# A two-layer decoder trunk on one core: 1/rms multiplied into U, another root and two banks for the last norm, the last two tiles stored one by one

## The chip, the core and the metric

The kernel runs on one core of a Trainium2 chip. TensorE (PE) multiplies matrices into eight PSUM banks, VectorE (DVE) and ScalarE (ACT) work on what comes out, GpSimd (POOL) helps with work that needs no PSUM, and SyncE (SP) issues most DMAs. Each engine takes its instructions from its own queue, in order, so an instruction that waits holds up all that stand behind it. The metric is the device time of one execution in microseconds, lower is better.

## The reference

The input `x` has 256 tokens of 1024 features. Two layers follow each other, each a mixer and an MLP, and a last norm ends the program:

```python
for layer in range(DEPTH):
    h = rms_norm(x, mix_norm[layer])
    x = x + (gdn_shortconv_mixer if layer % 2 == 0 else nsa_mixer)(h, ...)
    x = x + squared_relu_mlp(rms_norm(x, mlp_norm[layer]), w_up[layer], w_down[layer])
return rms_norm(x, final_norm)

def rms_norm(x, w):
    y = x * lax.rsqrt(jnp.mean(x * x, axis=-1, keepdims=True) + NORM_EPS)
    return y * w
def squared_relu_mlp(h, w_up, w_down):
    return jnp.square(jax.nn.relu(h @ w_up)) @ w_down
```

The MLP is 1024 to 4096 to 1024. Since relu is homogeneous, `relu((x*r) @ W)` is `relu(x @ W) * r` for the positive factor r = 1/rms of a token, and its square is `relu(x @ W)**2 * r**2`.

## The kernel before

Everything is held transposed, with features on the 128 partitions and the 256 tokens along a row: the residual stream `X` is eight tiles of 128x256. Precision is kept by splitting: each weight and each activation becomes a high part and a low part (`uh` and `ul` for the weights, `x[:, m, 0]` and `x[:, m, 1]` or `U[:, m, 0]` and `U[:, m, 1]` for the activations), and a product is three matmuls (`mm256`). A weight unit of 128x1024 is loaded by SP into a stage buffer (`st`), ACT copies it into `uh`, and DVE subtracts to get `ul` (for some units ACT and a DMA that accumulates do it). There are four unit buffers (`UB = 4`), so the split of a unit begins when PE is done with the unit four before it.

A norm does not wait with its result: PE multiplies by `x * w` without 1/rms, and the factor is applied behind. `Norm.ready(m)` splits a tile of `X` as it appears and squares it on ACT (`sq`), POOL or DVE adds the squares up (`nacc`). When the eighth is in, `Norm.finish` lets PE sum over the partitions with `ones`, DVE makes the mean (`ms`) and the root (`rsqrt`, eight small instructions on 128x2 numbers, result `ncol`), PE transposes the column into a row across all partitions (matmuls `b<-par,ncol`), and ACT copies that row out of PSUM (`rbc`). For the last norm (`self.last`) the sum is taken from `nacc` and the eighth `sq` apart, the bank of rows is kept (`n4.rows`), POOL has multiplied `X` by the weight beforehand, and `store` multiplies by the rows and issues the output DMAs in four groups of two tiles (`STORE`): groups on DVE read the bank, the group listed in `GST` runs on POOL and reads `rbc`.

In `mlp` the up projection makes 32 tiles of 128x256; the first four come together from `proj_ko`, the others one by one from `proj_m`. `evac` takes relu from PSUM on ACT (`t`), squares it (`u`), copies the high part to `U`, and DVE subtracts the low part. The down projection makes eight tiles of 96 matmuls each; `down` multiplies by `r2`, the square of `rbc`, and adds to `X`, two DVE instructions.

The order of every queue is fixed before the program runs: a small planner (`Order`) walks through all the streams with its own costs, picks the next instruction, and for some instructions picks the engine (a dict of engines after `yield`). So an edit in one place can change the order and the engines of everything that is planned later. In `mlp` and behind it, streams ask for a bank (`BANK`), for a token (`take`) or for a flag; `n.rbc` is there when the flag `norm1` or `norm3` is set.

Of the kernel before, what the change touches and what calls it, by code (L numbers as in the profile page):

```python
# [10 lines left out]
F32 = mybir.dt.float32  # L11
# [3 lines left out]
AF = mybir.ActivationFunctionType  # L15
# [5 lines left out]
T = 256  # L21
# [6 lines left out]
XBIAS, DBIAS, XB0 = 300, -400, 1e9  # L28
GM, GT, GO = 2, 1, 1
HEAD, CL = 0, 0  # L30
STORE, GST = (0, 2, 4, 6, 8), (2,)
FIRST, XS = (1,) * 8, ((1, 2), (2, 4), (4, 6), (6, 8))
PK, PW, PR, F1, GZ, ZP, LD, RT, P2 = 1, 1, 1, 1, 1, 1, 1, 21, 8
KPOOL, VPOOL, QPOOL, CVB = (), (), (0, 1, 2, 3), {'conv': 4, 'pool': 2}
# [129 lines left out]
class Order:  # L164
# [28 lines left out]
    def flag(self, name):  # L193
        self.flags.setdefault(name, self._now())
# [103 lines left out]
        self.t, self.last, self.hold = (parent.t, parent.last, parent.hold) if parent else (0.0, None, 0.0)  # L298


TABLES = {AF.Exp: ('e',), AF.Ln: ('l',), AF.Silu: ('s',), AF.Tanh: ('e', 's')}


class Timed:
# [61 lines left out]
BANK = ('bank',)  # L366
UB, SB, SPARE1 = 4, 8, 0
SLOTS, PTS = 4, 4
WARM, KEEP, KMAX = 11, 900.0, 8
ONE, WO, HALF, SOFT, TURN, VH = 1, 0, (0, 1), None, None, 1  # L370

# [17 lines left out]
def _build(ctx, nc, tc, wts, xin, parin, out, off):  # L389
# [380 lines left out]
    class Norm:  # L770
# [8 lines left out]
        def ready(self, m):  # L779
            w = self.w[:, m:m + 1]  # L780
            if self.acc is None:
                self.acc = tmp.tile([128, T], F32, name="nacc", bufs=1)
                if not self.last:
                    x = actp.tile([128, KT * 2 * T + 64], F32R, name="x")[:, 16:16 + KT * 2 * T]
                    self.x = x.rearrange("p (k a t) -> p k a t", k=KT, a=2)
            if not self.last:
                pick = yield dict(A=400, V=261 + (XBIAS if self.idx else XB0))
                if pick == 'A':
                    A.activation(self.x[:, m, 0], X[:, m], AF.Copy, scale=w)
                else:  # L790
                    V.tensor_scalar(self.x[:, m, 0], X[:, m], w, None, op0=OP.mult)
                yield 'V'
                V.scalar_tensor_tensor(self.x[:, m, 1], X[:, m], w, self.x[:, m, 0].bitcast(F32),
                                       op0=OP.mult, op1=OP.subtract)
                flag(f'n{self.idx}x{m}')
            self.begun += 1
            first = self.begun == 1
            if not first:
                yield 'take', 'sq', 3
            yield 'A'  # L800
            self.count += 1
            last = self.count == KT
            sq = self.acc if first else tmp.tile([128, T], F32, name="sq", bufs=3)
            A.activation(sq, X[:, m], AF.Square)
            if first:
                flag(f'n{self.idx}first')
            else:
                yield 'flag', f'n{self.idx}first'
                if last:
                    yield 'flag', f'n{self.idx}sum'  # L810
                    spawn(self.finish(sq), 0)
                else:
                    pick = yield dict(V=334) if not self.idx else dict(G=687)
                    (V if pick == 'V' else G).tensor_add(self.acc, self.acc, sq)
                    order.give('sq')
                    self.sums += 1
                    if self.sums == KT - 2:
                        flag(f'n{self.idx}sum')
            if self.last:
                yield 'G'  # L820
                G.tensor_mul(X[:, m], X[:, m], w.to_broadcast([128, T]))
                flag(f'xw{m}')

        def finish(self, sq):
            if not self.last:
                yield 'V'
                V.tensor_add(self.acc, self.acc, sq)
                order.give('sq')
            parts = [self.acc, sq] if self.last else [self.acc]
            yield 'flag', 'par2'  # L830
            ss = yield BANK
            yield 'PE'
            if self.last:
                keep(ss)
            for i, x in enumerate(parts):
                for t in range(2):
                    PE.matmul(ss[:, t:t + 1], x[:, t * 128:t * 128 + 128], ones, start=(t == 0 and i == 0),
                              stop=(t == 1 and x is parts[-1]))
            yield 'V'
            ms = tmp.tile([128, 2], F32, name="ms")  # L840
            V.tensor_scalar(ms, ss[:, :2], 1.0 / D, EPS, op0=OP.mult, op1=OP.add)
            release(ss)
            self.col = const.tile([128, 2], F32, name="ncol", bufs=2)
            rsqrt(self.col, ms, 2)
            flag(f'col{self.idx}')
            rb = yield BANK
            yield 'PE'
            if self.last:
                keep(rb)
            for t in range(2):  # L850
                PE.transpose(rb[:, t * 128:t * 128 + 128], self.col[:, t:t + 1].to_broadcast([128, 128]), ident)
            if self.last:
                self.rows = rb[:, :T]
                flag('rows')
            yield 'A'
            self.rbc = const.tile([128, T], F32, name="rbc", bufs=2)
            A.activation(self.rbc, rb[:, :T], AF.Copy)
            if not self.last:
                release(rb)
            flag(f'norm{self.idx}')  # L860

    def main():
        n0 = Norm(0)

        def start(m):
            yield 'flag', f'x{m}'
# [10 lines left out]
        n3 = Norm(3)  # L877
        yield from layer1(e, n2, n3)
        n4 = Norm(4, last=True)
        yield from mlp(e, n3, n4)  # L880

        def store(i, a, b):
# [19 lines left out]
def mlp(e, n, nxt):  # L902
    tc, tmp, X, order = e.tc, e.tmp, e.X, e.order
    V, A, PE, G = e.eng
    with tc.tile_pool(name="up", bufs=1) as up:
        U = up.tile([128, 32, 2, T], F32R, name="U")

        def evac(base):
            def f(m, acc):
                yield 'take', 'mlp', 3  # L910
                yield 'A'
                t = tmp.tile([128, T], F32, name="t", bufs=3)
                A.activation(t, acc[:, :T], AF.Relu)
                order.release(acc)
                u = up.tile([128, T], F32, name="u", bufs=3)
                A.activation(u, t, AF.Square)
                A.activation(U[:, base + m, 0], u, AF.Copy)
                yield 'V'
                V.tensor_sub(U[:, base + m, 1], u, U[:, base + m, 0].bitcast(F32))
                order.flag(f'U{n.idx}.{base + m}')  # L920
                order.give('mlp')
            return f

        yield from e.proj_ko(n, evac(0), wide=False)
        yield from e.proj_m(n.x, 28, evac(4))
        r2 = tmp.tile([128, T], F32, name="r2", bufs=1)

        def square():
            yield 'flag', f'norm{n.idx}'
            yield 'V'  # L930
            V.tensor_mul(r2, n.rbc, n.rbc)
            order.flag(f'r2.{n.idx}')

        order.spawn(square())

        def down(m, acc):
            yield 'flag', f'r2.{n.idx}'
            yield 'take', 'mlp', 3
            t = tmp.tile([128, T], F32, name="t", bufs=3)
            yield 'V'  # L940
            V.tensor_mul(t, acc[:, :T], r2)
            order.release(acc)
            V.tensor_add(X[:, m], X[:, m], t)
            order.give('mlp')
            order.spawn(nxt.ready(m))

        for m in range(KT):
# [1064 lines left out]
```

## Time and profile before

| what | us |
|---|---|
| median of three runs | 683.12 (681.45 to 685.27) |
| the profiled execution | 681.15 |
| its span, first to last instruction | 679.4 |
| PE busy in it | 659.2 |
| DVE, ACT, POOL busy | 455.9, 402.1, 119.9 |

The granted TensorE clock is 0.998 of full speed over the span. The stages by time from the start of the span: the first mixer to 182 us, the first MLP to about 356 us, attention to about 480 us, the second MLP to 668 us, and then the last norm and the output. Nearly all instructions are recorded by one helper, so they carry the line number L314 and are told apart by their tiles: `b` is any PSUM bank, `t<-b` the relu, `X<-X,b` a residual add or the last norm's multiplication.

### The profile page before, as it was taken

Reading aid. Unit: us, or ns where it says so; the run is one execution under the profiler, and the core shown is the slowest. Engines: PE = TensorE matmul, PEld = TensorE weight load, DVE = VectorE, ACT = ScalarE, POOL = GpSimd, SP = SyncE. Lnnn points to the kernel's source line nnn. Section 1 sums busy time; section 2 is a strip of 40 time slices with the busy share of each in tenths; the row PEclk is TensorE's granted clock in tenths of the full one; section 3 lists DMA queues with packets and bytes.
Section 4 is the critical chain, followed back from the end, with each engine's and each line's share of the span. In section 5 each row is a group of like instructions: output and inputs, shape, how many; then the busy total and the mean of one; then the engine's idle time right before and its main releaser. Section 6 shows DMA issues by size and latency. Waiting matters only on the chain.

```text
span 679.4 us, 16247 instructions
## 1 busy us (share of the span) xinstructions
PE 659.2 (97%) x6641; PEld 626.7 (92%) x6641; DVE 455.9 (67%) x871; ACT 402.1 (59%) x781; POOL 119.9 (18%) x159
## 2 busy tenths in 40 slices
PE   8999889999999999999999999998999999999995
PEld 6999789999999999999999877886899999999994
DVE  6999677586855655555557998887576555645552
ACT  7565223234888776444457678788578788544430
POOL 1001666410300000001033521021220000012121
PEclk9999999999999999999999999999999999999999
DMA  8961523136566666666658558362456555655401
GB/s 292 315 220 32 159 67 96 61 95 197 176 189 195 199 193 190 195 196 197 191 171 186 176 200 261 132 187 63 119 195 214 187 189 199 202 187 190 152 1 63
DMA packets 33770, 114.33 MB, mean 168 GB/s; under 512 B 3872, under 2 KB 4128, under 8 KB 33696
## 3 DMA queue, kind: packets, MB, share of 16 engines
q1 hardware_dynamic: 31968, 107.53, 50.4%
q0 software_dynamic: 1440, 5.24, 3.9%
q8 instruction: 52, 0.85, 0.5%
q10 hardware_dynamic: 288, 0.52, 0.2%
q14 instruction: 22, 0.18, 0.1%
HBM read 106.99 MB, written 1.05 MB: 159 GB/s over the span
## 4 chain that ended last, share of the span: by engine, by line
PE 80%; DVE 11%; ACT 4%; issue 2%; DMA 1%; SPq 0%; DVEq 0%; ACTq 0%
PE b L314 80%; DVE ul L314 3%; ACT uh L314 1%; DMA st<-wts 1%; ACT px L314 1%; DVE cvconv L314 1%; DVE rqt L314 1%; DVE kc L314 1%; DVE swq L314 1%; SPq L461 0%; DVE lc L314 0%; ACT E L314 0%; DVE qr L314 0%; DVE nm L314 0%; DVE preconv L314 0%
## 5 line engine op out<-in xcount | busy, mean ns | idle before, releaser
L314 DVE TENSOR_TENSOR ul<-st,uh 128x1024 fp32r<-128x1024 f32 (+3 forms) x194 | 228.2, 1179 | 152.7 <-ACT uh L314 150.8
L314 ACT ACTIVATE uh<-st 128x1024 fp32r<-128x1024 f32 (+3 forms) x204 | 206.4, 1013 | 200.9 <-PE b L314 166.6
L314 PE MATMUL b<-x,uh 128*128 128x256 f32 x1664 | 294.4, 281 | 0.6 <-issue 0.5
L314 PEld LDWEIGHTS b<-x,uh 128*128 128x128 f32 x1664 | 251.4, 188 | 3.7 <-issue 0.9
L314 PE MATMUL b<-x,ul 128*128 128x256 f32 x832 | 231.1, 278 | 1.6 <-DVE ul L314 1.1
L314 PE MATMUL b<-U,uh 128*128 128x256 f32 x1024 | 174.2, 276 | 0.0
L314 PEld LDWEIGHTS b<-x,ul 128*128 128x128 f32 x832 | 156.4, 188 | 2.8 <-DVE ul L314 2.1
L314 PEld LDWEIGHTS b<-U,uh 128*128 128x128 f32 x1024 | 154.0, 188 | 0.0
L314 PE MATMUL b<-U,ul 128*128 128x256 f32 x512 | 141.3, 276 | 0.0
L314 PEld LDWEIGHTS b<-U,ul 128*128 128x128 f32 x512 | 96.1, 188 | 0.0
L314 POOL TENSOR_TENSOR nacc<-nacc,sq 128x256 f32<-128x256 f32 x24 | 29.9, 1246 | 242.4 <-ACT sq L314 241.9
L314 ACT ACTIVATE px<-b,nm 128x128 f32<-128x128 f32 (+1 forms) x64 | 26.6, 440 | 3.5 <-DVE nm L314 3.4
L314 ACT ACTIVATE U<-u 128x256 fp32r<-128x256 f32 x64 | 26.8, 419 | 2.0
L314 ACT ACTIVATE u<-t 128x256 f32<-128x256 f32 x64 | 26.7, 418 | 2.0
L314 DVE TENSOR_TENSOR U<-u,U 128x256 fp32r<-128x256 f32 x64 | 27.0, 424 | 0.7 <-ACT U L314 0.7
L314 PE MATMUL b<-uh,x 128*128 128x264 f32 (+1 forms) x128 | 24.5, 288 | 0.0
L314 PE MATMUL b<-ohl,uh 128*128 128x256 f32 x128 | 23.9, 287 | 0.2
L314 ACT ACTIVATE t<-b 128x256 f32<-128x256 f32 x64 | 23.3, 364 | 0.0
L314 POOL TENSOR_TENSOR X<-X,par 128x256 f32<-128x256 f32 x8 | 5.5, 691 | 100.8 <-ACT nacc L314 91.8
L314 PEld LDWEIGHTS b<-uh,x 128*128 128x128 f32 x128 | 20.3, 188 | 0.0
L314 PEld LDWEIGHTS b<-ohl,uh 128*128 128x128 f32 x128 | 19.5, 188 | 0.7 <-ACT ohl L314 0.3
L314 ACT ACTIVATE sq<-X 128x256 f32<-128x256 f32 x35 | 13.5, 404 | 10.6 <-DVE X L314 10.5
(275 smaller groups left out, 797.6 us busy)
## 6 DMA issues: line engine op xcount, KB each, us to landing
st<-wts SPq DMA_DIRECT2D x188, 512.0 KB, 3.7
ul<-st POOLq DMA_DIRECT2D x10, 512.0 KB, 4.8
st<-wts SPq DMA_DIRECT2D x8, 280.0 KB, 2.9
st<-wts SPq DMA_DIRECT2D x8, 264.0 KB, 5.9
st<-wts SPq DMA_DIRECT2D x8, 256.0 KB, 6.3
X<-xt SPq DMA_DIRECT2D x3, 256.0 KB, 6.1
par<-par SPq DMA_DIRECT2D x1, 525.0 KB, 6.7
out_dram<-X SPq DMA_DIRECT2D x2, 256.0 KB, 2.6
```

The costliest lines, as they stand in the source:

```text
L314: r = f(*a, **k)
```

## The change

It has three parts. In `mlp`, relu and the product with 1/rms become one DVE instruction that reads the bank and `n.rbc`, so `U` holds the finished activation; `r2` and its product go, and `down` is one addition from the bank. In the last norm, the root is a DVE reciprocal, an ACT `Sqrt`, and one Newton step of three DVE instructions; `ACT` loads the table for `Sqrt` early, in a stream `root` that waits for `norm3`; and the row across partitions is made twice, in two banks, one for DVE and one for ACT's copy. In `store`, the last group of two tiles becomes two groups of one. (Two constants, `SQ0` and `NA0`, are brought in with the values that the code had.)

```diff
-STORE, GST = (0, 2, 4, 6, 8), (2,)
+STORE, GST = (0, 2, 4, 6, 7, 8), (2,)
...
+SQ0, NA0 = 'A', dict(V=334)
...
 # Norm.finish
-            rsqrt(self.col, ms, 2)
+            if self.last:
+                y = tmp.tile([128, 16], F32, name="rqt", bufs=3)
+                V.reciprocal(y[:, :2], ms)
+                yield 'A'
+                A.activation(y[:, 2:4], y[:, :2], AF.Sqrt)
+                yield 'V'
+                V.tensor_mul(y[:, 4:6], y[:, 2:4], y[:, 2:4])
+                V.scalar_tensor_tensor(y[:, 4:6], y[:, 4:6], -0.5, ms, op0=OP.mult, op1=OP.mult)
+                V.scalar_tensor_tensor(self.col, y[:, 4:6], 1.5, y[:, 2:4], op0=OP.add, op1=OP.mult)
+            else:
+                rsqrt(self.col, ms, 2)
...
             if self.last:
                 self.rows = rb[:, :T]
                 flag('rows')
+                rb = yield BANK
+                yield 'PE'
+                for t in range(2):
+                    PE.transpose(rb[:, t * 128:t * 128 + 128], self.col[:, t:t + 1].to_broadcast([128, 128]), ident)
...
+        def root():
+
+            yield 'flag', 'norm3'
+            yield 'A'
+            A.activation(tmp.tile([128, 1], F32, name="tb", bufs=3), ones, AF.Sqrt)
...
 # mlp
                 yield 'take', 'mlp', 3
+                yield 'flag', f'norm{n.idx}'
+                yield 'V'
+                t = tmp.tile([128, T], F32, name="t", bufs=3)
+                V.scalar_tensor_tensor(t, acc[:, :T], 0.0, n.rbc, op0=OP.max, op1=OP.mult)
+                order.release(acc)
                 yield 'A'
-                t = tmp.tile([128, T], F32, name="t", bufs=3)
-                A.activation(t, acc[:, :T], AF.Relu)
-                order.release(acc)
...
         def down(m, acc):
-            yield 'flag', f'r2.{n.idx}'
-            yield 'take', 'mlp', 3
-            t = tmp.tile([128, T], F32, name="t", bufs=3)
             yield 'V'
-            V.tensor_mul(t, acc[:, :T], r2)
+            V.tensor_add(X[:, m], X[:, m], acc[:, :T])
             order.release(acc)
-            V.tensor_add(X[:, m], X[:, m], t)
-            order.give('mlp')
             order.spawn(nxt.ready(m))
```

The first place is the start of the second MLP, right behind the root of its norm. DVE's queue there, before (`ul` is the low part of a weight unit, `U` the low part of an activation tile):

```order
L314 SCALAR_TENSOR_TENSOR ncol<-rqt,ncol 128x2
L314 TENSOR_TENSOR U<-u,U 128x256 x3
L314 TENSOR_TENSOR ul_7108<-st,uh_7107 128x1024
L314 TENSOR_TENSOR U<-u,U 128x256
L314 TENSOR_TENSOR ul_7150<-st,uh_7149 128x1024
```

The same place of DVE's queue with the change, where `t<-b,rbc` is the new instruction:

```order
L314 SCALAR_TENSOR_TENSOR ncol<-rqt,ncol 128x2
L314 TENSOR_TENSOR ul_7075<-st,uh_7074 128x1024
L314 SCALAR_TENSOR_TENSOR t<-b_6903,rbc 128x256
L314 SCALAR_TENSOR_TENSOR t<-b_6904,rbc 128x256
L314 SCALAR_TENSOR_TENSOR t<-b_6905,rbc 128x256
L314 TENSOR_TENSOR ul_7117<-st,uh_7116 128x1024
L314 TENSOR_TENSOR U<-u,U 128x256 x2
L314 SCALAR_TENSOR_TENSOR t<-b_6906,rbc 128x256
L314 SCALAR_TENSOR_TENSOR t<-b_7067,rbc 128x256
L314 TENSOR_TENSOR ul_7155<-st,uh_7154 128x1024
```

Before, three tiles had been taken out of PSUM by ACT and stood ready for their subtraction; now the first three leave PSUM here, behind `rbc`, and their subtractions come a unit later. ACT's queue at this place, with the change:

```order
L314 ACTIVATE uh_7074<-st 128x1024
L314 ACTIVATE rbc<-b_7077 128x256
L314 ACT_TABLE_LOAD
L314 ACTIVATE tb<-ones 128x1
L314 ACTIVATE uh_7116<-st 128x1024
L314 ACTIVATE u<-t 128x256
L314 ACTIVATE U<-u 128x256
L314 ACTIVATE u<-t 128x256
L314 ACTIVATE U<-u 128x256
L314 ACTIVATE uh_7154<-st 128x1024
```

The table load and the first `Sqrt` stand between `rbc` and the next weight unit; there is no table load behind them to the end of ACT's queue.

The second place is the end of the program. DVE's last instructions before (the branch that ends the queue left out):

```order
L314 TENSOR_TENSOR t<-b_9027,r_8141 128x256
L314 TENSOR_TENSOR X<-X,t 128x256
L314 TENSOR_SCALAR ms<-b_9140 128x2
L314 TENSOR_SCALAR ncol<-ms 128x2
L314 TENSOR_TENSOR rqt<-ncol 128x2
L314 TENSOR_TENSOR rqt<-rqt,ms 128x2
L314 SCALAR_TENSOR_TENSOR rqt<-rqt 128x2
L314 SCALAR_TENSOR_TENSOR ncol<-rqt,ncol 128x2
L314 TENSOR_TENSOR rqt<-ncol 128x2
L314 SCALAR_TENSOR_TENSOR rqt<-rqt,ms 128x2
L314 SCALAR_TENSOR_TENSOR ncol<-rqt,ncol 128x2
L314 TENSOR_TENSOR X<-X,b_9163 128x512 x3
```

With the change (`rqt<-ms` is the reciprocal; ACT's `Sqrt` stands between it and the next):

```order
L314 TENSOR_TENSOR X<-X,b_8996 128x256
L314 TENSOR_SCALAR ms<-b_9106 128x2
L314 RECIPROCAL rqt<-ms 128x2
L314 TENSOR_TENSOR rqt<-rqt 128x2
L314 SCALAR_TENSOR_TENSOR rqt<-rqt,ms 128x2
L314 SCALAR_TENSOR_TENSOR ncol<-rqt 128x2
L314 TENSOR_TENSOR X<-X,b_9124 128x512 x2
L314 TENSOR_TENSOR X<-X,b_9124 128x256 x2
```

One instruction for the last residual tile instead of two, five on DVE and one on ACT for the root instead of nine on DVE, and four multiplications instead of three; they read another bank (`b_9124`) than ACT's copy (`b_9131`).

The third place is attention, which the planner lays out anew although none of its code changed. DVE's queue shortly behind the root of layer 1's first norm, before (`rtab`, `sw`, `kst` are the rotary embedding of the keys, `QQ` and `qrot` that of the queries, `KD` and `KL` the two parts of the keys):

```order
L314 TENSOR_SCALAR rtab<-rope 128x512
L314 STREAM_SHUFFLE sw<-kst 128x256 x2
L314 COPY QQ<-b_5141 128x256
L314 TENSOR_TENSOR qrot<-QQ,rtab 128x256
L314 TENSOR_TENSOR ul_5192<-st,uh_5191 128x1024
L314 TENSOR_TENSOR sw<-sw,rope 128x256
L314 TENSOR_TENSOR kst<-kst,sw 128x256
```

The same place with the change:

```order
L314 TENSOR_SCALAR rtab<-rope 128x512
L314 STREAM_SHUFFLE sw<-kst 128x256 x2
L314 TENSOR_TENSOR sw<-sw,rope 128x256
L314 TENSOR_TENSOR kst<-kst,sw 128x256
L314 TENSOR_TENSOR ul_5175<-st,uh_5174 128x1024
L314 CAST KD<-kst 64x256
```

The copy and the product of the queries have left DVE here, and the keys come ahead of the weight unit. From here to the end of attention the queues of all engines differ in order, and some instructions have changed engines, while the matmuls are the same in number.

## Rows read from the trace of the kernel before

**Rows 1.** The page: busy time by engine; the chain that ended last, by engine.

```profile
PE 659.2 (97%) x6641; PEld 626.7 (92%) x6641; DVE 455.9 (67%) x871; ACT 402.1 (59%) x781; POOL 119.9 (18%) x159
...
PE 80%; DVE 11%; ACT 4%; issue 2%; DMA 1%; SPq 0%; DVEq 0%; ACTq 0%
```

**Rows 2.** Windows by stage: PE, PEld, DVE, ACT, POOL busy (count); clock, DMA share, GB/s.

```profile
182.00:356.00 174.00, 173.57 (x1529) 173.23 (x1529) 100.44 (x133) 109.47 (x176) 12.65 (x15) 1.00 0.65 190
369.00:480.00 111.00, 106.79 (x824) 88.03 (x822) 91.51 (x246) 85.62 (x256) 23.31 (x39) 1.00 0.56 164
480.00:668.00 188.00, 187.92 (x1658) 187.91 (x1658) 107.54 (x141) 111.92 (x181) 20.97 (x20) 1.00 0.51 166
668.00:679.40 11.40, 3.95 (x24) 2.24 (x22) 4.19 (x14) 0.80 (x2) 1.88 (x2) 0.85 0.25 92
```

**Rows 3.** Waits of PE from 369 to 480 us: total us, times, longest.

```profile
PE b L314 <- DVE qr L314: 1.0, 1, 1.0
PE b L314 <- DVE pc L314: 0.9, 1, 0.9
PE b L314 <- ACT px L314: 0.7, 1, 0.7
PE b L314 <- ACT pts L314: 0.6, 2, 0.3
PE b L314 <- DMA ul<-st: 0.5, 1, 0.5
```

**Rows 4.** Timeline from 668 us, by engine: start, us, what, idle time before.

```profile
668.41 0.42 DVE L314 TENSOR_TENSOR t<-b,r 128x256 f32<-128x256 f32 x1 [8.67 <-PE b L314]
668.87 0.42 DVE L314 TENSOR_TENSOR X<-X,t 128x256 f32<-128x256 f32 x1
669.39 0.42 ACT L314 ACTIVATE sq<-X 128x256 f32<-128x256 f32 x1 [10.46 <-DVE X L314]
...
670.50 0.16 DVE L314 TENSOR_SCALAR ms<-b 128x2 f32<-128x2 f32 x1 [1.21 <-PE b L314]
...
672.08 0.16 DVE L314 SCALAR_TENSOR_TENSOR ncol<-rqt,ncol 128x2 f32<-128x2 f32 x1
672.30 0.43 PE L314 MATMUL b<-par,ncol 128*128 128x128 f32 x2 [0.73 <-DVE ncol L314]
672.77 0.38 ACT L314 ACTIVATE rbc<-b 128x256 f32<-128x256 f32 x1 [2.96 <-PE b L314]
673.25 1.88 DVE L314 TENSOR_TENSOR X<-X,b 128x512 f32<-128x512 f32 x3 [1.01 <-ACT rbc L314]
```

**Rows 5.** Groups by line and shape: count, busy us, mean ns, idle before.

```profile
L314 ACT ACTIVATE t<-b 128x256 f32<-128x256 f32 x64 | 23.3, 364 | 0.0
L314 DVE SCALAR_TENSOR_TENSOR hid<-hid,b 128x256 f32<-128x256 f32 x1 | 0.4, 407 | 0.0
L314 DVE RECIPROCAL den<-den 128x8 f32<-128x8 f32 x8 | 1.6, 194 | 0.7 <-ACT px L314 0.7
L314 ACT ACTIVATE tb<-ones 128x1 f32<-128x1 f32 x1 | 0.2, 203 | 0.0
L314 ACT ACT_TABLE_LOAD x3 | 3.8, 1283 | 0.8 <-PEq L2001 0.7
```

**Rows 6.** Timeline at the start of the second MLP, DVE and ACT.

```profile
505.44 0.16 DVE L314 SCALAR_TENSOR_TENSOR ncol<-rqt,ncol 128x2 f32<-128x2 f32 x1
...
511.71 1.23 DVE L314 TENSOR_TENSOR ul<-st,uh 128x1024 fp32r<-128x1024 f32 x1 [0.52 <-ACT uh L314]
...
507.06 0.37 ACT L314 ACTIVATE rbc<-b 128x256 f32<-128x256 f32 x1
...
513.26 1.06 ACT L314 ACTIVATE uh<-st 128x1024 fp32r<-128x1024 f32 x1 [0.41 <-PE b L314]
```

**Rows 7.** Tile `out_dram`: the four output DMAs of 256 KB, issue to landing.

```profile
DMA to landing us min/median/max: 2.3/2.9/3.3
```

**Rows 8.** Window of the output, columns as in group 2.

```profile
674.80:677.70 2.90, 0.00 (x0) 0.00 (x0) 0.33 (x1) 0.00 (x0) 0.00 (x0) 0.71 0.97 362
```

More of the change, by code (lines that the diff above doesn't have):

```diff
@@ L298, in __init__ @@
         self.t, self.last, self.hold = (parent.t, parent.last, parent.hold) if parent else (0.0, None, 0.0)
-TABLES = {AF.Exp: ('e',), AF.Ln: ('l',), AF.Silu: ('s',), AF.Tanh: ('e', 's')}
+TABLES = {AF.Exp: ('e',), AF.Ln: ('l',), AF.Silu: ('s',), AF.Tanh: ('e', 's'), AF.Sqrt: ('q',)}
 class Timed:
@@ L799, in ready @@
                 yield 'take', 'sq', 3
-            yield 'A'
+            pick = yield SQ0 if not self.idx else 'A'
             self.count += 1
@@ L803, in ready @@
             sq = self.acc if first else tmp.tile([128, T], F32, name="sq", bufs=3)
-            A.activation(sq, X[:, m], AF.Square)
+            if pick == 'A':
+                A.activation(sq, X[:, m], AF.Square)
+            else:
+                G.tensor_mul(sq, X[:, m], X[:, m])
             if first:
@@ L812, in ready @@
                 else:
-                    pick = yield dict(V=334) if not self.idx else dict(G=687)
+                    pick = yield NA0 if not self.idx else dict(G=687)
                     (V if pick == 'V' else G).tensor_add(self.acc, self.acc, sq)
@@ L843, in finish @@
             self.col = const.tile([128, 2], F32, name="ncol", bufs=2)
-            rsqrt(self.col, ms, 2)
+            if self.last:
[7 more added lines that the diff above has]
+                V.scalar_tensor_tensor(self.col, y[:, 4:6], 1.5, y[:, 2:4], op0=OP.add, op1=OP.mult)
+            else:
+                rsqrt(self.col, ms, 2)
             flag(f'col{self.idx}')
@@ L879, in main @@
         n4 = Norm(4, last=True)
+        spawn(root())
         yield from mlp(e, n3, n4)
@@ L925, in mlp, with down @@
         yield from e.proj_m(n.x, 28, evac(4))
-        r2 = tmp.tile([128, T], F32, name="r2", bufs=1)
-        def square():
-            yield 'flag', f'norm{n.idx}'
+        def down(m, acc):
             yield 'V'
[L931 to L936, printed above, removed]
-            yield 'flag', f'r2.{n.idx}'
-            yield 'take', 'mlp', 3
-            t = tmp.tile([128, T], F32, name="t", bufs=3)
-            yield 'V'
-            V.tensor_mul(t, acc[:, :T], r2)
+            V.tensor_add(X[:, m], X[:, m], acc[:, :T])
             order.release(acc)
-            V.tensor_add(X[:, m], X[:, m], t)
-            order.give('mlp')
             order.spawn(nxt.ready(m))
```

## The prediction, made before the changed kernel ran

> **What bounds the kernel now.** I read the page first, then windows by stage, then the waits of PE where it waits, then the timeline of the last 12 us. On the page PE is busy for 97% of the span and holds 80% of the chain that ended last [rows 1]. The windows say where that is not so [rows 2]. In the first MLP PE is busy for 173.57 of 174 us, in the second for 187.92 of 188: nothing that ACT or DVE does there is on the path as long as it is in time. In attention PE is idle for 111 - 106.79 = 4.2 us, of which named waits account for 1.0 + 0.9 + 0.7 + 0.6 + 0.5 = 3.7 us [rows 3]. From 668 us on PE has little to do, and 11.4 us go by in one chain: last residual add, squares, sum, root, rows, multiplication, output [rows 4, 7, 8]. The reader is to see that this chain is the one place where an edit of this change moves the end directly.
>
> **The end of the program, step by step.** *Residual add.* The last tile takes `t` at 668.41 and `X` at 668.87 [rows 4]; with one addition from the bank, the square on ACT starts as far behind the first instruction as it now does behind the second, so 668.87 - 668.41 = 0.46 us is gained. (Ends, here and below, are a row's start plus its duration.) A DVE instruction that reads a bank and a tile takes as long as one that reads two tiles (both 0.42), so nothing is given back.
>
> *Root.* Now it is 672.30 - 670.50 = 1.80 us from `ms` to the transposes, with one instruction every (672.08 - 670.50) / 8 = 0.20 us [rows 4]. With the change: `ms` 0.20; the reciprocal, for which the trace has 0.19 for 128x8 [rows 5] and 0.16 for other instructions on 128x2, so 0.17; a hand-over from DVE to ACT of 669.39 - 669.29 = 0.10; the `Sqrt`, for which the nearest is a 128x1 activation of 0.20 [rows 5]; a hand-over from ACT to DVE of 673.25 - 673.15 = 0.10; three instructions 0.20 + 0.20 + 0.16; and 672.30 - 672.24 = 0.06 to PE [rows 4]. That is 1.39, a gain of 0.41. Bounds: 0.19 if the `Sqrt` takes as long as an activation of 256 numbers (0.42), 0.5 if each hand-over takes half.
>
> *Two banks.* DVE's multiplication starts 673.25 - 672.30 = 0.95 us behind the transposes, and what ended its wait is ACT's copy `rbc` out of the same bank, not PE [rows 4]. From a bank of its own it starts 0.43 (the transposes) + 0.04 (PE to ACT there, 672.77 - 672.73) behind, a gain of 0.48. Lower bound: if the second pair of transposes has to end first, another 0.43 is waited for, and 0.05 is left. ACT's copy and POOL's product behind it come up to 0.43 later against the transposes; meanwhile the DMA engines have the bytes of DVE's groups.
>
> *Stores.* 1 MB of output moves from 674.80 to 677.70 at 362 GB/s with the 16 DMA engines 97% busy [rows 8]. So the landing of the last byte follows from the start of the first group and the bytes, not from when the last group is issued, and I take the split at 0. Bounds: DVE takes four instructions in place of three (1.88 us [rows 4]), and if two halves of 0.42 stand for one of 0.63, the last issue is 0.2 later, a loss of 0.2; a gain of 0.3 if the last, smaller DMA lands like the one that was alone (2.3 instead of the longest's 3.3 [rows 7], of which the shared engines leave a part).
>
> The Trainium skill, in "DMA: Bandwidth & Descriptors", section "Anatomy of one DMA — SWDGE (gpsimd) path", speaks against the split: each DMA (of GpSimd's path, for which it gives the figures) costs about 2.0 us fixed plus its bytes over 436 GB/s. By it a 256 KB store takes 2.6 us and a 128 KB store 2.3, a gain of 0.3 for the last; the trace has 2.3 to 3.3 for four equal ones, so here the queueing decides and not the fixed part.
>
> The sum is 0.46 + 0.41 + 0.48 + 0 = 1.35 us, bounds 0.46 + 0.19 + 0.05 - 0.2 = 0.5 and 0.46 + 0.5 + 0.48 + 0.3 = 1.75.
>
> **The MLPs.** 64 relus leave ACT, 23.3 us at 364 ns; 64 instructions come to DVE at about 0.41 (the one row of that operation from a bank at this size, 407 ns [rows 5]), 26 us, less 16 products of 0.42, 7 us. Per up tile, 24 matmuls at 188 / 1658 = 0.113 us [rows 2], so 2.72 us, DVE then has 1.23 (`ul`) + 0.42 + 0.41 = 2.06 to do and ACT 1.06 + 0.42 + 0.42 = 1.90: both fit, so I take nothing. The new wait is on 1/rms. Behind the first waiting `t` in DVE's queue stand the next `ul` and the subtractions for `U`, and PE waits for those and for banks. *Banks:* the root ends at 505.60 [rows 6]; PE is then in its fifth tile (the built order has the transposes in its middle), half of it is still to come, then three tiles have banks (one free, the sum's, the rows'), and the ninth tile is the first to need one of the four: 1.36 + 3 x 2.72 = 9.5 us later, 515.1. `rbc` ends at 507.43, so a first bank is free at 507.9. Cover: 7 us. *Weights:* the copy at 513.26 was waiting for PE to leave a buffer [rows 6]; that buffer is wanted three tiles later, at 521.4, and the split takes 1.06 + 1.23, so it has 5.8 us to spare. Put ahead of it by the new order are three `t` (1.3 us) and, on ACT, a table load and a small activation (1.28 + 0.20 [rows 5]): 2.8 us. Without that cover each further microsecond would be one of PE's.
>
> The Trainium skill, in "ScalarE: Activation LUTs", section "What ACT_TABLE_LOAD costs", counts 2.66 us for a switch, 1283 ns for the load and the rest for a drain, and tells to batch by set. The rows have 1283 ns for the load. By the page ACT would be late by 1.4 more, 4.2 of 5.8, and the sum the same.
>
> **Attention** is planned anew. Rows cannot say which way that goes; the nearest bounds are that all of PE's named waits vanish (-3.7 us [rows 3]) or come twice (+3.7). I take 0, since matmuls are equal in number and DVE, which is busy for 91.5 of 111 us [rows 2], loses about as much as it gets.
>
> **Rivals.** *Attention gains.* DVE and PE both end its waits [rows 3], and at the place shown the queries leave DVE early. With three quarters of 3.7 gained, 2.7, the time falls 4.1 us; against it, every wait is under 1 us and has its own cause. *Attention loses, and it is slower.* Place: the score matmuls that wait for `qr` and the copies of `px`. It decides where PE's 3.7 us of waits grow by more than the 1.35 gained; at twice as much the time is 2.35 us above before, and 4.8 us more are needed for 0.5%. *The MLPs stall.* If the root were 7 us late for banks, or the splits 5.8 us for weights, PE stops in both MLPs; 2.5 us beyond that in each is 5 - 1.35 = 3.6 slower. The rows speak against it. *The last chain does not shorten as it says.* If DVE still waits for ACT's bank or PE's second pair, and the root's hand-overs are long, 0.5 us is gained.
>
> **How the numbers follow.** The profiled execution took 681.15, with a span of 679.4; 1.35 off makes 679.8. It lies below the three timed runs (median 683.12); the four together average 682.75, and 1.35 off that is 681.4, which I give. Chances: attention near 0 and the end shortened 0.66; attention gains 0.17 (682.75 - 4.1 = 678.7); attention loses 0.08 (up to 685.1); MLPs stall 0.04 (686.4); the end hardly shortened 0.05 (682.2). For 8 in 10 the range reaches to both attention cases, and a little below the first, for runs that fall like the fastest: 677.3 to 685.1. What a measurement tells from no change is about 0.5%, 3.4 us. The forecast is within it; the first rival is mostly beyond: faster 0.19, same 0.74, slower 0.07.
>
> **What would show it.** From the last matmul with `U` to the end it should be 1.35 us shorter: the square 0.46 earlier, `ms` to transposes about 1.4, transposes to DVE's product about 0.5 with PE as its releaser, the output window as dense as now. In both MLPs PE should have no gap at the ninth tile. A changed distance between the first and the second MLP's start is attention's. Wrong would be a PE wait on `t` or `ul` in an MLP, a table load in the last 12 us, or attention off by over 3 us.

## The result and the profile after

The changed kernel takes 677.98 us (median of eight runs, 676.54 to 680.62), the kernel before 682.79 in the runs beside it (681.03 to 685.51): a ratio of 0.9932, interval 0.9904 to 0.9959, so about 4.6 us less. That is faster, clear of noise: by 0.7% at the median, and by at least 0.4% by the interval. It is inside the forecast's range, 3.4 us below the forecast, and 0.7 us from the first rival, that attention gains. The range holds it because it was drawn around both attention cases; the case on which the forecast rests, attention near 0, did not come.

The page of the changed kernel, busy time by engine and the chain that ended last, answers to [rows 1]:

```profile
PE 658.2 (97%) x6639; PEld 628.8 (93%) x6640; DVE 474.2 (70%) x914; ACT 375.6 (55%) x717; POOL 126.3 (19%) x162
...
PE 82%; DVE 8%; ACT 4%; issue 2%; DMA 2%; SPq 0%; DVEq 0%; ACTq 0%
```

The profiled execution took 678.94 us, its span is 677.1. DVE is busy for 18 us more and ACT for 27 less, as the relu has moved from one to the other, but DVE's share of the chain has gone down. The windows by stage, as in [rows 2]:

```profile
182.00:356.00 174.00, 173.72 (x1533) 173.55 (x1532) 114.28 (x169) 93.97 (x138) 13.65 (x15) 1.00 0.64 192
369.00:480.00 111.00, 108.36 (x846) 91.79 (x846) 90.67 (x240) 87.31 (x258) 26.14 (x42) 1.00 0.56 167
480.00:668.00 188.00, 187.91 (x1656) 187.60 (x1655) 115.42 (x165) 100.38 (x151) 22.27 (x21) 1.00 0.50 166
```

The MLPs are as full as before. Attention is not the same: in the same 111 us PE is busy 1.6 us longer and gets 22 more matmuls done. Since fixed windows cut stages at different places, I measure attention from PE's last `b<-U` of the first MLP to its last `b<-ohl`, the output projection's last matmul. The timeline of PE at the two ends, of the kernel before:

```profile
346.81 0.28 PE L314 MATMUL b<-U,ul 128*128 128x256 f32 x1
...
493.28 0.28 PE L314 MATMUL b<-ohl,ul 128*128 128x256 f32 x1
```

and of the changed one:

```profile
347.92 0.28 PE L314 MATMUL b<-U,ul 128*128 128x256 f32 x1
...
491.58 0.28 PE L314 MATMUL b<-ohl,ul 128*128 128x256 f32 x1
```

So attention has gone from 493.28 - 346.81 = 146.47 us to 143.66, with 1133 matmuls between the marks in both: 2.8 us, the largest part of the gain. Between the marks PE is idle for 4.3 us before and 2.6 after, and the same matmuls keep it busy for 142.2 us before and 141.0 after, so 1.6 us of the gain is idle time and 1.2 is matmuls that take less. PE's named waits from 369 to 480 us (total us, times, longest) have gone from 3.7 [rows 3] to 2.4:

```profile
PE b L314 <- DMA ul<-st: 1.2, 2, 0.9
PE b L314 <- ACT pts L314: 1.0, 2, 0.7
PE b L314 <- ACT px L314: 0.2, 1, 0.2
```

The end of the program, the timeline by engine, answers to [rows 4]:

```profile
666.40 0.28 PE L314 MATMUL b<-U,ul 128*128 128x256 f32 x1
...
666.71 0.42 DVE L314 TENSOR_TENSOR X<-X,b 128x256 f32<-128x256 f32 x1 [8.67 <-PE b L314]
...
667.23 0.42 ACT L314 ACTIVATE sq<-X 128x256 f32<-128x256 f32 x1 [10.14 <-DVE X L314]
...
668.34 0.16 DVE L314 TENSOR_SCALAR ms<-b 128x2 f32<-128x2 f32 x1 [1.21 <-PE b L314]
668.53 0.17 DVE L314 RECIPROCAL rqt<-ms 128x2 f32<-128x2 f32 x1
668.73 0.20 ACT L314 ACTIVATE rqt<-rqt 128x2 f32<-128x2 f32 x1 [1.09 <-DVE rqt L314]
668.97 0.16 DVE L314 TENSOR_TENSOR rqt<-rqt 128x2 f32<-128x2 f32 x1 [0.27 <-ACT rqt L314]
...
669.58 0.65 PE L314 MATMUL b<-par,ncol 128*128 128x128 f32 x4 [0.39 <-DVE ncol L314]
670.12 1.95 DVE L314 TENSOR_TENSOR X<-X,b 128x512 f32<-128x512 f32 x4 [0.60 <-PE b L314]
670.26 0.38 ACT L314 ACTIVATE rbc<-b 128x256 f32<-128x256 f32 x1 [1.33 <-PE b L314]
670.79 1.27 POOL L314 TENSOR_TENSOR X<-X,rbc 128x512 f32<-128x512 f32 x1 [2.46 <-ACT rbc L314]
```

Here the reader sees all three shortenings: one residual addition, 668.34 to 669.58 for the root, and DVE's product waiting for PE and no more for ACT. The last matmul with `U` ends at 666.68 here and at 668.37 before. Measured from there, DVE's product starts at 3.44 us and at 4.88 before, 1.44 earlier; but the span ends at 10.46 and 11.00 before, only 0.54 earlier. The 0.9 between is lost behind the product: the last output DMA lands at 9.12 and at 10.10 before, 0.98 earlier, so 0.46 is lost up to there, and 0.44 more behind it. The window of the output, columns as in [rows 2], answers to [rows 8]; the two lines below it divide it:

```profile
671.65:675.25 3.60, 0.00 (x0) 0.00 (x0) 0.41 (x2) 0.00 (x0) 0.41 (x1) 0.81 0.83 294
...
671.70:674.50 2.80, 0.00 (x0) 0.00 (x0) 0.36 (x2) 0.00 (x0) 0.36 (x1) 0.89 1.01 361
674.50:675.24 0.74, 0.00 (x0) 0.00 (x0) 0.00 (x0) 0.00 (x0) 0.00 (x0) 0.50 0.15 47
```

The same 1 MB is spread over 3.6 us at 294 GB/s, with the DMA engines 83% busy, where it was 2.9 us at 362 and 97%. But the engines are full until 674.50, at 361 GB/s (packets overlap a little, so the share can pass 1); what pulls the mean down is a tail of 0.74 us, from about 674.8 on with one packet under way at a time. A queue and the output DMAs in the last 6 us (KB each, median us from issue to landing):

```profile
q14 instruction: 1, 0.01, 0.5%
...
out_dram<-X SPq DMA_DIRECT2D x2, 256.0 KB, 2.9
out_dram<-X ACTq DMA_DIRECT2D x1, 256.0 KB, 2.6
out_dram<-X ACTq DMA_DIRECT2D x1, 128.0 KB, 3.5
out_dram<-X SPq DMA_DIRECT2D x1, 128.0 KB, 3.3
```

The three DMAs that are issued last take 3.3 to 3.5 us, the two small ones and POOL's of 256 KB (the other on SP takes 2.4). `q14 instruction` is a fetch of 8 KB of instructions, which runs in the middle of the output, 6.73 us behind the last `U` matmul. And at the very end SP's queue waits for its DMAs; before:

```profile
SPq L2007 <- DMA out_dram<-X: 3.1, 3, 1.2
```

and after:

```profile
SPq L2020 <- DMA out_dram<-X: 2.8, 1, 2.8
```

Before, SP waits for landings three times, one after the other; after, its first wait of 2.8 us ends with the DMA that lands last, and all its other waits stand behind it: eight in all, from 675.82 to 676.25, one every 0.06 us. The last landing is at 675.80, the span ends 1.34 us later; before, it was 0.90.

### The profile page after: what moved, and what is told of

It is laid out like the page before. It is cut to its first block, busy times and chain, and to the rows that moved or that the text cites. A ratio compares the mean times of both kernels' runs of the same rounds, so it can differ in the third digit from the quotient of the medians.

```text
span 677.1 us, 16199 instructions
## 1 busy us (share of the span) xinstructions
PE 658.2 (97%) x6639; PEld 628.8 (93%) x6640; DVE 474.2 (70%) x914; ACT 375.6 (55%) x717; POOL 126.3 (19%) x162
## 4 chain that ended last, share of the span: by engine, by line
PE 82%; DVE 8%; ACT 4%; issue 2%; DMA 2%; SPq 0%; DVEq 0%; ACTq 0%
PE b L314 82%; DVE ul L314 3%; ACT uh L314 1%; DMA ul<-st 1%; DMA X<-xt 1%; DVE cvconv L314 1%; DMA st<-wts 1%; ACT ul L314 1%; DVE lc L314 0%; DVE rqt L314 0%; ACT E L314 0%; DVE nacc L314 0%; SPq L462 0%; DVE preconv L314 0%; DVE al L314 0%
## 5 line engine op out<-in xcount | busy, mean ns | idle before, releaser
L314 POOL TENSOR_TENSOR nacc<-nacc,sq 128x256 f32<-128x256 f32 x24 | 32.4, 1351 | 237.2 <-ACT sq L314 227.5
L314 DVE SCALAR_TENSOR_TENSOR t<-b,rbc 128x256 f32<-128x256 f32 x64 | 26.6, 424 | 8.3 <-PE b L314 8.3
L314 ACT ACTIVATE px<-b,nm 128x256 f32<-128x256 f32 (+1 forms) x64 | 26.4, 429 | 3.6 <-DVE nm L314 3.5
L314 DVE TENSOR_TENSOR X<-X,b 128x256 f32<-128x256 f32 (+1 forms) x28 | 13.9, 514 | 16.3 <-PE b L314 16.3
```

Of the source, the lines that this page charges most:

```text
L314: r = f(*a, **k)
```

## The experiments

Lengths of two stages in one profile of each, in us: attention between the marks above, and the end, from the end of the last matmul with `U` to the end of the span. From the same matmul are counted the start of DVE's first product and the last landing of an output DMA; "fetch" tells whether an instruction fetch of 8 KB ran while the output moved. Ratios are to the kernel before, with their 95% interval, where runs were timed.

| kernel | attention | product | last landing | end | fetch | ratio |
|---|---|---|---|---|---|---|
| before | 146.47 | 4.88 | 10.10 | 11.00 | no | 1 |
| changed | 143.66 | 3.44 | 9.12 | 10.46 | yes | 0.9932 [0.9904, 0.9959] |
| tail_only | 146.48 | 3.91 | 9.14 | 10.47 | no | 0.9976 [0.9960, 0.9993] |
| mlp_only | 144.19 | 4.41 | 9.63 | 10.64 | no | 0.9942 [0.9926, 0.9958] |
| store4 | 143.62 | 3.44 | 8.93 | 9.83 | yes | |
| one_bank | 143.69 | 3.86 | 9.29 | 10.45 | yes | |
| old_root | 143.66 | 3.99 | 9.23 | 10.68 | no | |
| out4 | 143.71 | 3.44 | 8.75 | 9.66 | yes | |
| before_d4400 | 147.99 | 4.87 | 10.09 | 10.99 | no | |
| before_d4600 | 144.01 | 4.87 | 10.09 | 10.99 | no | |
| before_d4600_t | 144.33 | 4.87 | 10.10 | 10.99 | no | 0.9959 [0.9945, 0.9973] |
| after_d4300 | 139.73 | 3.44 | 8.69 | 10.14 | no | |
| after_d4600 | 145.77 | 3.44 | 8.66 | 10.00 | no | |
| best | 140.71 | 3.44 | 8.48 | 9.49 | no | 0.9875 [0.9851, 0.9899] |

The stages of the changed kernel add up to 2.8 + 0.5 + 0.3 (the first MLP, below) = 3.6 us, within the 2.8 to 6.6 of the ratio's interval. The second MLP, from the last `b<-ohl` to the end of the last matmul with `U`, is 175.1 us in all of them. The first mixer, whose queues are the same in all, varies from 182.9 to 187.3 us, and by 4 us between two profiles of one kernel (187.25 in `before_d4600`, 183.27 in `before_d4600_t`). So the time of one execution can't tell 2 us, and I compare stages, and timed runs where there are some.

**tail_only**: `mlp` as before; last norm and stores as changed. To the end of attention its queues are those of the kernel before, and PE's to the last norm.

```diff
-                V.scalar_tensor_tensor(t, acc[:, :T], 0.0, n.rbc, op0=OP.max, op1=OP.mult)
+                A.activation(t, acc[:, :T], AF.Relu)
...
+            V.tensor_mul(t, acc[:, :T], r2)
             order.release(acc)
```

> The last norm's root and two banks and the split stores, with the MLPs as before. All queues up to the last residual add stand as before, so attention is laid out as before. If the gain of the whole change is attention's new order (2.8 us from the last matmul with U to the last with ohl in the two traces), this one gains little: the end becomes 0.54 - 0.46 = about 0.1 us shorter than before, attention stays at 146.5 us, ratio 0.999 to 1.001. If the gain comes from the end of the program, it should be near 0.995.

Measured: attention 146.48, the end 10.47, 0.53 shorter than before. Timed, 0.5 to 2.7 us less than 682.5 (ratio 0.9960 to 0.9993). Without the new MLP code attention's gain is gone. The 0.1 us and the ratio of 0.999 to 1.001 that were expected are missed: the end gained less in the changed kernel's profile, from which they were subtracted, than it does here.

**mlp_only**: `mlp` as changed; last norm and stores as before. To the end of attention its queues are those of the changed kernel.

```diff
-            if self.last:
-                y = tmp.tile([128, 16], F32, name="rqt", bufs=3)
...
+            rsqrt(self.col, ms, 2)
...
-STORE, GST = (0, 2, 4, 6, 7, 8), (2,)
+STORE, GST = (0, 2, 4, 6, 8), (2,)
```

> 1/rms multiplied into U and one residual addition, with the last norm and the stores as before. All queues up to the last residual add stand as in the changed kernel. If attention's new order is the gain: attention 143.7 us as in the changed kernel, first MLP from sums to sums about as before, the end 0.46 shorter through the residual add, 3.3 to 4.5 us off in all, ratio 0.993 to 0.996. If the end of the program is the gain: ratio 0.999.

Measured: attention 144.19, ratio 0.9942, most of the whole change's 0.9932. The end is 0.36 shorter, and the last landing 0.47 earlier; the residual addition's share was forecast at 0.46. Where the edit to the MLPs goes, the gain goes, though it falls in attention and not in the MLPs.

**before_d4400, before_d4600, after_d4300, after_d4600**: no code is changed, only a constant of the planner, its estimate in ns for the DMAs that make the low part of some weight units (4500 in both kernels). It moves nothing but the order from attention on, and in `before_d4400` adds five matmuls with zeros (`b<-zeros`) to it.

```diff
-BYDMA, DLAT = (*range(113, 121, 2), *range(129, 141, 2)), 4500
+BYDMA, DLAT = (*range(113, 121, 2), *range(129, 141, 2)), 4600
```

> The kernel before with one planner constant changed (DLAT, the time that the planner allows for a split by DMA, 4500 to 4400): the queues differ within attention alone, the work is the same. From the last matmul with U of the first MLP to the last with ohl the kernel before takes 146.5 us, the changed kernel 143.7. If attention's gain is only another draw of the planner: here too it moves by 1 us or more, to anywhere between 143 and 149 us. If the edit of the MLPs gives attention something of its own: it stays at 146.5, within 0.5.

> The kernel before with DLAT at 4600: another order in attention. If the gain is a draw of the planner: 143 to 149 us, another value than 146.5. If it is the MLP edit's own: 146.5 within 0.5.

> The changed kernel with DLAT at 4300, which reorders attention alone. If the gain is a draw: anywhere between 143 and 149 us, and with luck shorter than 143.7. If it is the MLP edit's own: 143.7 within 0.5.

> The changed kernel with DLAT at 4600. If the gain is a draw: another value between 143 and 149 us. If it is the MLP edit's own: 143.7 within 0.5.

Measured: with the code of before, attention takes 148.0, 146.5 and 144.0 us at 4400, 4500 and 4600; with the changed code 139.7, 143.7 and 145.8 at 4300, 4500 and 4600. Neither code has the shorter attention throughout, and the direction of the constant is opposite in the two. The changed kernel's 143.7 is one draw out of a spread of 8 us.

What three orders of each code don't show is that the edit has no share of its own in attention. Their means are 146.2 us with the code of before and 143.1 with the changed code, and the two ranges overlap. One thing differs in all the profiles by the code and not by the constant: the sum for the root of layer 1's first norm, PE's `b<-ones,nacc`, begins 8.3 us after the mark at which attention begins in each of the five with the MLPs of before and 6.2 us after it in each of the nine with the new ones. Before and after:

```profile
355.08 0.50 PE L314 MATMUL b<-ones,nacc 128*128 128x1 f32 x4
...
354.16 0.50 PE L314 MATMUL b<-ones,nacc 128*128 128x1 f32 x4
```

What those 2 us are worth in attention, no run shows. The same queues also differ from one execution to another, by 0.3 us (`before_d4600` and `before_d4600_t`), 0.5 (the changed kernel and `mlp_only`) and 1.0 (`after_d4300` and `best`).

**before_d4600_t**: the same kernel as `before_d4600`, timed.

> The kernel before with nothing of the change, only the planning constant at 4600 for 4500, timed. If most of the change's gain is the new order of attention, an order drawn by that constant alone gives as much: attention 144.0 us against 146.5, ratio 0.9955 to 0.9975, with end and MLPs as before. If the gain comes from the code of the MLPs and the end, the ratio is 0.999 to 1.001.

Measured: 679.60 us, ratio 0.9959, interval 0.9945 to 0.9973. With none of the change's code the kernel gains 2.8 us, 1.8 to 3.8 by the interval; its attention is 2.1 us shorter than before in this profile. PE's waits from 330 to 500 us in it:

```profile
PE b L314 <- DVE qr L314: 1.1, 1, 1.1
PE b L314 <- ACT pts L314: 1.0, 2, 0.7
PE b L314 <- DMA ul<-st: 0.4, 1, 0.4
PE b L314 <- ACT px L314: 0.2, 1, 0.2
```

Against [rows 3] the wait on DVE's `pc` is gone and that on `px` is shorter. In the changed kernel `qr` is gone too, and the wait on the low part by DMA (`ul<-st`) has grown. So each order has other waits, with other releasers; there is no one wait which the change removes.

**store4**: the changed kernel with four groups of two tiles.

```diff
-STORE, GST = (0, 2, 4, 6, 7, 8), (2,)
+STORE, GST = (0, 2, 4, 6, 8), (2,)
```

> The whole change with the stores in four groups of two as before. The changed kernel's output window is 3.56 us against 2.90 before, and SP goes through eight waits in 0.43 us after the last landing. If the split is what stretched it: from the first product of DVE to the end 0.5 to 1.0 us less than the 7.02 us of the changed kernel, and the landing of the longest DMA last in SP's row of waits. If POOL's group, which now comes late against DVE's, is the cause: about the same 7.0 us.

Measured: the end is 9.83, 0.63 shorter than with the split (10.46): the last landing is 0.19 earlier, and 0.90 instead of 1.34 follow it. The longest DMA's landing now ends the last of SP's waits. With the split the end is 10.14 and 10.00 in `after_d4300` and `after_d4600`, where no fetch falls into the output, so the split costs 0.2 to 0.6 us. Against before, four groups and the rest of the change gain 1.17.

**out4**: the changed kernel with four groups of 1, 2, 2 and 3 tiles (the third on POOL).

```diff
-STORE, GST = (0, 2, 4, 6, 7, 8), (2,)
+STORE, GST = (0, 1, 3, 5, 8), (2,)
```

> The whole change with four groups of another size: tiles 0, 1 to 2, 3 to 4 on POOL, and 5 to 7. One DMA fewer than in the changed kernel, and the first is issued behind one tile. If the number of DMAs decides about SP's row of waits: 0.9 us from the last landing to the end, as before and with four equal groups, against 1.34 in the changed kernel. If the size of the last group decides: 1.3. If the first byte sets the end, the data begins 0.27 earlier than with four equal groups (5.00 behind the last matmul with U) and ends 0.2 to 0.3 earlier than its 8.50; if POOL's group or the last one sets it, 8.4 to 8.6.

Measured: the end is 9.66, again 0.2 less than with equal groups, and 0.8 less than with the split. From the last landing to the end it is 0.91. The data begins 0.26 earlier than with equal groups (4.74 for 5.00) and ends 0.17 earlier (8.33 for 8.50), so neither the first byte nor the last group alone sets the end. In these profiles a small group helps at the front, where it makes the first issue earlier (3.89 us behind the last `U` matmul for 4.16), not at the back.

**one_bank**: the changed kernel with one bank of rows for DVE and ACT, as before.

```diff
-                rb = yield BANK
-                yield 'PE'
-                for t in range(2):
-                    PE.transpose(rb[:, t * 128:t * 128 + 128], self.col[:, t:t + 1].to_broadcast([128, 128]), ident)
```

> The whole change with one bank of rows. If DVE's product waits for ACT's copy because both read one bank: 0.95 us again from the first transpose to DVE's product, against 0.54 in the changed kernel. If the wait is on PE or on something else: about 0.5. POOL's product starts 0.2 to 0.3 us earlier against the transposes, so the output window is denser than the changed kernel's 3.56 us and the end gains back a part.

Measured: DVE's product waits for ACT again,

```profile
671.00 1.95 DVE L314 TENSOR_TENSOR X<-X,b 128x512 f32<-128x512 f32 x4 [1.01 <-ACT rbc L314]
```

and starts 0.96 us behind the transposes, where it was 0.54 with two banks: the second bank gains 0.42 there. But the last landing is only 0.17 later than with two banks and the end, 10.45, is the same, so here those 0.42 are not in the end of the span. POOL's group comes earlier against the transposes with one bank, as ACT copies without waiting for a second pair.

**old_root**: the changed kernel with the root of before.

```diff
-                V.reciprocal(y[:, :2], ms)
-                yield 'A'
-                A.activation(y[:, 2:4], y[:, :2], AF.Sqrt)
...
+            rsqrt(self.col, ms, 2)
```

> The whole change with the root as before (eight small DVE instructions, no Sqrt, no table load). From ms to the first transpose the kernel before takes 1.79 us and the changed one 1.24. If the new root is what shortens it: 1.79 here. If the end is then bound by the output and not by this chain: the last landing comes less than 0.3 us later against the last matmul with U than the changed kernel's 9.12.

Measured: from `ms` at 668.54 to the transposes at 670.33 it is 1.79, and 1.24 with the new root, so the root gains 0.55. The end is 10.68, 0.22 longer than with the new root, and the last landing 0.11 later (9.23 for 9.12), which would mean that the output binds. But a fetch falls into the output of the changed kernel and not into this one. Against `after_d4300` and `after_d4600`, which have none and whose code differs from this one's in the root and the constant alone, the last landing is 0.54 and 0.57 later and the end 0.54 and 0.68: there the root's 0.55 goes through to the end.

**best**: the changed kernel with the constant at 4300 and the groups of `out4`, timed.

> The changed kernel with one planning constant set lower (4300 for 4500, the estimated delay of the DMA that builds a low part) and the output in four groups of 1, 2, 2 and 3 tiles. If the order of attention and the stores are worth in timed runs what the single profiles of those variants showed, then attention is about 139.7 us long (143.7 with the changed kernel, 146.5 before), the time from the last U matmul to the end of the span about 9.7 (10.5 and 11.0), and the ratio to before is 0.985 to 0.989. If the order of attention is only a draw whose gain does not repeat, the ratio stays at 0.992 to 0.994, as the change alone has it.

Measured: 673.46 us (672.71 to 675.74), ratio 0.9875, interval 0.9851 to 0.9899; it beats both kernels. Attention is 140.71 (139.73 with the same queues in `after_d4300`), the end 9.49. PE's waits from 330 to 500 us have come down to two kinds:

```profile
PE b L314 <- DMA ul<-st: 1.1, 2, 0.7
PE b L314 <- ACT px L314: 0.4, 1, 0.4
```

Its output DMAs, in the window from 660 us, land in

```profile
out_dram<-X ACTq DMA_DIRECT2D x1, 384.0 KB, 3.1
...
out_dram<-X SPq DMA_DIRECT2D x1, 128.0 KB, 1.9
```

The stages add up: 146.47 - 140.71 = 5.8 in attention, 1.5 at the end, 0.3 in the first MLP, together 7.6 of the 8.5 (6.9 to 10.2) that the ratio gives.

## Why the prediction was right and wrong

**Attention, taken at 0, was the step that failed.** It gained 2.8 us, and that is what put the time near the first rival (2.7 in attention, 678.7 us; measured 677.98). The gain comes with an order which the planner drew: `mlp_only` has it, `tail_only` has not, and `before_d4600_t` has nearly as much with none of the edit. So an order alone can give it; whether the edit has a share besides, through its earlier root, is open. That the rival's size fits is luck: its 2.7 was three quarters of PE's 3.7 us of named waits (2.8, worked out), of which 1.3 went, and it counted on 1.35 at the end, where 0.54 came. That DVE's load hardly changes in the stage (91.51 to 90.67 us busy) was foreseen, and it did not matter: what counts is which waits are met.

The bounds of that step, plus or minus the 3.7 us of PE's named waits, were made wrongly too. `after_d4300` is 6.7 us shorter than before, more than all those waits. PE's rows are not all of it: 1.2 us of the gain is in the time for which the same matmuls keep PE busy, and the weight loads (`PEld`) have rows of waits of their own. From 369 to 480 us, of the kernel before:

```profile
PEld b L314 <- ACT pts L314: 2.2, 6, 0.6
...
PEld b L314 <- ACT px L314: 1.7, 3, 1.1
PEld b L314 <- ACT KD L314: 1.1, 1, 1.1
PEld b L314 <- ACT pct L314: 0.9, 1, 0.9
```

and of the changed one:

```profile
PEld b L314 <- DMA ul<-st: 1.6, 2, 1.1
PEld b L314 <- ACT pts L314: 1.3, 4, 0.8
...
PEld b L314 <- ACT px L314: 0.7, 2, 0.5
```

The named ones sum to 8.5 us before and 4.8 after, 3.7 less. PE and `PEld` are both busy for over 90% of the span, so loads and matmuls overlap and this is no sum of lost time, but a bound from these rows would have held all the orders. That these waits make up the rest of the 2.8 beyond PE's own (3.7 - 2.4 = 1.3) is argued from the rows, not shown by a run.

**The chain at the end** went as forecast up to DVE's product: 0.46 for the residual addition (forecast 0.46), 0.55 for the root (0.41), 0.41 for the banks (0.48), 1.44 in all against 1.35. The root's error is in the hand-overs: from the `Sqrt`'s start to the next DVE instruction it is 668.97 - 668.73 = 0.24, where 0.20 + 0.10 had been taken, and from the reciprocal's start to the `Sqrt` 0.20, where 0.17 + 0.10 had been. The second pair of transposes held DVE up by no more than 0.07 (0.54 against the forecast 0.47).

**The stores, taken at 0 with bounds -0.2 and +0.3, were the second step that failed**: 1.44 gained by the product became 0.54 at the end of this span, and 0.86 and 1.00 in the two other profiles with the same code there. The loss is in two places, one on either side of the last landing:
- Up to the last landing, 0.46. The sentence that the last landing follows from the start of the first group and the bytes holds where no instruction fetch falls into the output: against before, product and landing are earlier by 0.97 and 0.96 us in `tail_only`, 0.47 and 0.47 in `mlp_only`, 0.89 and 0.87 in `old_root`, 1.44 and 1.41 in `after_d4300`, 1.44 and 1.44 in `after_d4600`. In the four profiles with the fetch the landing gains less than the product, by 0.46 in the changed kernel, 0.27 in `store4`, 0.21 in `one_bank` and 0.09 in `out4`, which has a smaller first group. The fetch takes 0.45 us in the changed kernel and 0.31 to 0.33 in the others, and a tail of single packets ends each of them. That it is the cause is argued from this; no run moved it alone, and in the changed kernel ACT also issues its 128 KB 0.27 later than in `after_d4300`, with DVE's products at the same times.
- Behind the last landing, 0.44, a term that the sum did not have. The landing of a fifth DMA is the one that SP's row of waits asks for first. Where it lands last, seven more waits at 0.06 us follow it; with four DMAs the last landing ends the last wait that asks for one. With five, the span ends 1.16 to 1.45 us behind the last landing (six profiles: the changed kernel, `tail_only`, `one_bank`, `old_root`, `after_d4300`, `after_d4600`), the shortest in `one_bank`, where another DMA lands last; with four, 0.89 to 1.02 (the eight others). In `after_d4300` and `after_d4600` all of the loss is here, 0.55 and 0.43; what adds 0.1 in some of the profiles is open.

POOL's group, which had been issued right behind the second, does come late: the groups are issued at 4.15, 4.75, 5.41 (POOL's), 5.45 and 5.84 us behind the last `U` matmul, where the four issues of before lie at 5.59, 6.19, 6.21 and 6.78, because ACT's copy waits for the second pair. The forecast that the bytes of DVE's groups cover this holds: the engines are full until 674.50.

The gain of up to 0.3 that the upper bound had for a smaller last DMA did not come. The two DMAs of 128 KB take 3.5 and 3.3 us to land, and 2.5 and 2.8 in `after_d4300`. The Trainium skill, in "DMA: Bandwidth & Descriptors", section "Anatomy of one DMA — SWDGE (gpsimd) path", by which 2.3 us was worked out for 128 KB (an estimate), is not borne out for these, which SP and ACT issue: the trace has 3.5 and 3.3, while the 128 KB that `best` sends first, with nothing ahead, land in 1.9.

**The MLPs** were taken at 0 and gain 0.3 in the first (from the start of the last matmul of its norm's sum to the end of the last with `U` 164.17 us before, 163.86 after): PE had waited 0.2 for `ncol` behind that norm, and does no more. From 480 us to the last norm PE has no wait in the changed kernel. The new instruction takes 424 ns, where 407 had been taken from one row:

```profile
L314 DVE SCALAR_TENSOR_TENSOR t<-b,rbc 128x256 f32<-128x256 f32 x64 | 26.6, 424 | 8.3 <-PE b L314 8.3
```

The table load stands where the order had it, and costs what the row of before gave. ACT's timeline there:

```profile
505.22 1.28 ACT L314 ACT_TABLE_LOAD   x1
506.52 0.20 ACT L314 ACTIVATE tb<-ones 128x1 f32<-128x1 f32 x1
506.62 1.05 ACT L314 ACTIVATE uh<-st 128x1024 fp32r<-128x1024 f32 x1
```

The Trainium skill, in "ScalarE: Activation LUTs", section "What ACT_TABLE_LOAD costs", counts 2.66 us for a switch. The trace agrees with the 1283 ns for the load and has no drain: `rbc` ends at 505.21 and the load begins at 505.22, and the next activation follows 0.02 behind it.

So the forecast of 681.4 was of the case in which attention stays, and the nearest thing to a run of that case, `tail_only`, took 681.04, though its stages account for only 0.5 of the 1.35 that was forecast. The chance of 0.17 for the first rival looks too small: over six orders on the two codes, four of them drawn by nothing but a constant moved by 2 to 4%, the stage's length ranged from 139.7 to 148.0 us, six times what I gave to the end of the program.

## What to carry to other kernels

Where a planner lays out a stage anew, its length is drawn again whatever the edit was for: before an edit is credited, draw the order of the old code anew as well, by a constant that means nothing, and compare each stage by marks on the engine that bounds it. Bound such a draw by the waits of the weight loads as well as of the matmuls. At the end of a program follow the chain to the last instruction of the span: a product that starts 1.4 us earlier can bring the last landing forward by as much and the end by 0.4 less, if the landing that comes last is the one that is waited for first. In these profiles a small store paid at the front and not at the back. Before two ends are compared, look whether the same foreign transfers fall into both.

## What the runs showed of the hardware

- After the last landing the span goes on for 0.89 to 1.45 us. In the changed kernel the longest DMA's landing (675.80) ended SP's first wait (675.82), and seven more waits went by one after the other, to 676.25, some 0.06 us each.
- An instruction fetch of 8 KB (the row `q14 instruction` above) fell into the output in the changed kernel, `store4`, `one_bank` and `out4`, and into none of the other ten. With the same code at the end, the last landing is 9.12 us behind the last `U` matmul with it and 8.69 and 8.66 without.
- Four stores of 256 KB moved at 362 GB/s with the 16 engines 97% busy, and five stores, two of them of 128 KB, at 361 GB/s until the tail.
- The same queues of the first mixer took 182.9 to 187.3 us in these profiles, with a mean granted clock of 0.989 to 0.998 of full speed over the whole span. In the two longest (`before_d4600` and `before_d4400`) the clock granted from 60 to 100 us is 0.91 of full speed, where the kernel before has 1.00 and the changed one 0.96; `tail_only`, at 1.00 all through the first mixer, took 184.6, so the clock is not all of it, and the rest stays open.
